# A hybrid decoder layer: order of sums, casts and low parts in the down projections, and place of two norm matmuls

## The chip, the cores and the metric

The kernel runs on one core of a Trainium2 chip. The metric is the time of one execution on the device in microseconds (us), lower is better. Times are medians of several runs.

## The reference, cut to what matters

One inference step of a decoder layer with two feed-forward blocks around a mixing part, in float32, for 1048 tokens (16 learned, 1024 of the prompt, 8 samples) and a model width of 1024:

```
h = h + 0.5 * swiglu(rmsnorm(h, n1), w1g, w1u, w1d)
u = rmsnorm(h, nm) @ w_in
...                      (two scans over u, one output projection)
h = h + 0.5 * swiglu(rmsnorm(h, n2), w2g, w2u, w2d)

def swiglu(x, wg, wu, wd):
    return (jax.nn.silu(x @ wg) * (x @ wu)) @ wd
```

`wg` and `wu` are 1024 x 2816, `wd` is 2816 x 1024. The change concerns the products with `wd`, the two **down phases**, and the norm that follows the first of them.

## The kernel before

**One product in three.** A float32 matmul is done as three in a reduced format (`mm3`, L140 to L145): each operand is split into a high part, the cast of it (L137, on ACT, the scalar engine), and a low part, operand minus high part (L138, on DVE, the vector engine). The three products are high by high (L143), high by low (L144) and low by high (L145), 262 columns (a quarter of the tokens) each. The low part needs the cast, so DVE waits for ACT each time.

**Seven products in place of eight.** `down` (L529) multiplies 2 by 2 blocks with seven products after Strassen and Winograd. Blocks of the weight are its even and odd row tiles by its even and odd column tiles (11, 12, 21, 22), blocks of the hidden activations are token quarters. The products p run in the order 1, 5, 6, 7, 3, 4, 2 (`DORDER`, L468). Four of them need sums of weight blocks (L563): S1 = 21 + 22 for p=5, S2 = S1 - 11 for p=6, S3 = 11 - 21 for p=7, S4 = 12 - S2 for p=3. S1, S2 and S4 share one kept buffer, each written over the one before; S3 is made in the raw buffer of block 11. Sums of activation blocks were stored to DRAM earlier and come back as operands (`Hidden.load`, L509, transfers u<-hd).

**Steps.** The phase is a list of steps on PE (the tensor engine), 24 for each product: four pairs of output tiles j, three groups of weight rows g (4, 4 and 3 tiles of 128), two halves c of the tokens. A step has 12 or 9 matmuls. A **piece** is the weight of one (p, j, g); it serves two steps, and b is the first of them. In the last product (p=2) the order is c, j, g: a piece has one step in each half, pieces are one step apart, and the last six pieces live in larger "u" buffers. `S.before(i, f)` (L286 to L307) puts f ahead of step i. Within `manual_schedule` (L626 and after) the order in which these functions run is the order of the instructions on each engine and on SP, the queue that issues the DMAs. So the numbers in `S.before` are the plan: an engine works through its list in order, waits where data are missing, and runs ahead of PE where nothing holds it.

For a piece: loads at b-13 (L553, raw buffers, 8 of them), the sum, where there is one, at b-8, cast and low part at b-7 (L566 to L568). The split weights lie in 6 buffers "ws" (L71). For an operand: load, then cast and low part in one step s, for most products s = b-16+3m for its six parts m.

**Ends.** After the last step of a pair j, DVE adds 0.5 times the result to the residual stream h (L582): 4 such evacuations in p=1, 2 in p=5, 3 in p=6, 2 in p=7, 1 in the others. PE has two accumulators "acc", so tile j+2 waits for the evacuation of tile j. Where a block of h is final and a norm follows (first phase, from p=3 on), ACT squares it (L198, L201) and POOL (GpSimd) adds the squares up (L202). `Norm.end(q)` (L204 to L209) lets PE add the squares of quarter q over the partitions (matmul with ones, L209), ACT and DVE make the reciprocal root from it (L159 to L163). In the first phase quarters 1 and 3 are final after p=3. `after1` puts their `nm.end` at e3+2 and e3+4 (L1432), where e3 is the first step of p=4. In the second phase no such norm follows; output tiles are transposed and written instead.

Of the kernel before, what the change touches and what calls it, by code (L numbers as in the profile page):

```python
# [9 lines left out]
F32 = mybir.dt.float32  # L10
F32R = mybir.dt.float32r
U8 = mybir.dt.uint8
AF = mybir.ActivationFunctionType
ALU = mybir.AluOpType
# [3 lines left out]
P = 128  # L18
# [194 lines left out]
def new_x(K):  # L213
    K.xhi, K.xlo = ([K.slot("u", T, F32R) for k in range(KT)] for i in range(2))
# [133 lines left out]
def product(K, ps, w, op, n, first, last, more=False):  # L348
    for k in range(n):
        ks = slice(k * Q, k * Q + Q)  # L350
        wh, wl = (w[:, o + k * P : o + k * P + P] for o in (0, 512))
        K.mm3(ps, wh, wl, op[0][:, ks], op[1][:, ks], first and k == 0, last and k == n - 1, more)
# [119 lines left out]
class Hidden:  # L472
# [36 lines left out]
    def load(self, S, p, at):  # L509

        K = self.K
        op = [{}, {}]

        def load(g, c):
            i, n = GROUPS[g]
            op[c][g] = K.slot("u", n * Q, F32R), K.slot("u", n * Q, F32R)
            K.nc.sync.dma_start(op[c][g][1].bitcast(F32), self.d[p][:, c, i : i + n].rearrange("p n t -> p (n t)"))

        def split(g, c):
            hi, lo = op[c][g]  # L520
            K.split(lo.bitcast(F32), hi, lo)

        for (g, c), l, s in zip([(g, c) for g in range(3) for c in range(2)], *at):
            S.before(l, lambda g=g, c=c: load(g, c))
            S.before(s, lambda g=g, c=c: split(g, c))
        return op


def down(K, S, wdv, hidden, src, h, after):  # L529

    nc = K.nc
    s0 = len(S.steps)
    hs = []
    sums, w = {}, {}

    def load_h(o):
        t = K.slot("s", T)
        nc.sync.dma_start(t, src(o))
        h.append(t)
        hs.append(t.rearrange("p (c n t) -> p c n t", c=2, n=2))  # L540

    for o in range(KT):
        S.before(s0 + (-4, 2, 8, 9)[o // 2], lambda o=o: load_h(o))

    def pieces(p, j, g, b, tag):

        i0, n = GROUPS[g]
        raw = {}

        def load(a):  # L550
            i, o = {11: (0, 0), 12: (1, 0), 21: (0, 1), 22: (1, 1)}[a]
            raw[a] = K.raw(n * P)
            nc.sync.dma_start(raw[a].rearrange("p (k c) -> p k c", k=n), wdv[:, 2 * i0 + i : 2 * (i0 + n) : 2, (2 * j + o) * P : (2 * j + o) * P + P])  # L553

        def val(x):
            return raw[x] if x in raw else sums[j, g]

        def sum_(x, y, op):
            if p == 5:
                if (j % 2, g) == (0, 0):  # L560
                    sums["slots"] = [K.slot("u", 1024) for _ in range(3)]
                sums[j, g] = sums["slots"][g][:, j % 2 * 512 : j % 2 * 512 + n * P]
            nc.vector.tensor_tensor(raw[11] if p == 7 else sums[j, g], val(x), val(y), op)  # L563

        def split():
            t = K.ws() if tag is None else K.slot(tag, 1024, F32R)  # L566
            w[p, j, g] = K.split_w(val({1: 11, 7: 11, 4: 22, 2: 12}.get(p, 0)), t)

        for a in {1: (11,), 5: (21, 22), 6: (11,), 7: (11, 21), 3: (12,), 4: (22,), 2: (12,)}[p]:
            S.before(b - 13, lambda a=a: load(a))  # L570
        if p in (5, 6, 7, 3):
            x, y = {5: (21, 22), 6: (0, 11), 7: (11, 21), 3: (12, 0)}[p]
            S.before(b - 8, lambda: sum_(x, y, ALU.add if p == 5 else ALU.subtract))
        S.before(b - 7, split)

    def matmuls(p, j, g, c, op, ps):
        product(K, ps, w[p, j, g], op[c][g], GROUPS[g][1], g == 0, g == 2)

    def post(p, j, cs, b):
        for i, n in {1: ((0, 0), (0, 1), (1, 0), (1, 1)), 5: ((0, 1), (1, 1)), 6: ((0, 1), (1, 0), (1, 1)), 7: ((1, 0), (1, 1)), 3: ((0, 1),), 4: ((1, 0),), 2: ((0, 0),)}[p]:  # L580
            t = hs[2 * j + i][:, cs, n]
            nc.vector.scalar_tensor_tensor(t, b, 0.5, t, ALU.mult, ALU.add)  # L582
        for i, n in {3: ((0, 1), (1, 1)), 4: ((1, 0),), 2: ((0, 0),)}.get(p, ()):
            if then:
                for c in range(cs.start, cs.stop):
                    then(2 * j + i, 2 * c + n)

    for a, p in enumerate(DORDER):
        b = s0 + 24 * a
        if a == 0:  # L590
            at = [b + k for k in (-14, -11, -11, -9, -9, -7)], [b + k for k in (-8, -7, -6, -5, -4, -2)]
        else:
            at = [b - 22 + 3 * m for m in range(6)], [b - 16 + 3 * m for m in range(6)]
        op = hidden.load(S, p, at)
        if a < 6:
            for j in range(KT // 2):
                box = []
                for g in range(3):
                    pieces(p, j, g, b + 6 * j + 2 * g, None)
                    for c in range(2):  # L600

                        def mm(p=p, j=j, g=g, c=c, op=op, box=box):
                            if not box:
                                box.append(K.psum2()[:, :, :Q])
                            matmuls(p, j, g, c, op, box[0][:, c])

                        S.add(mm, (lambda p=p, j=j, box=box: post(p, j, slice(0, 2), box[0])) if (g, c) == (2, 1) else None)
        else:
            then = after(S, h, b - 48 + 24, b + 12, b + 24)
            for j in range(KT // 2):  # L610
                for g in range(3):
                    pieces(p, j, g, b + 3 * j + g, None if j < 2 else "u")
            for c in range(2):
                for j in range(KT // 2):
                    box = []
                    for g in range(3):

                        def mm(p=p, j=j, g=g, c=c, op=op, box=box):
                            if not box:
                                box.append(K.psum()[:, :Q])  # L620
                            matmuls(p, j, g, c, op, box[0])

                        S.add(mm, (lambda p=p, j=j, c=c, box=box: post(p, j, slice(c, c + 1), box[0][:, None])) if g == 2 else None)
# [768 lines left out]
def body(ctx, tc, a, o):  # L1392
    nc = tc.nc
    K = Core(ctx, tc)
# [5 lines left out]
    x = Input(K, a, wn1, ops)  # L1400
# [12 lines left out]
    def after1(S, h, e3, e0, e1):  # L1413
        nm = Norm(K, h)
# [14 lines left out]
                nc.sync.dma_start(hsp[k * P : (k + 1) * P, cs], h[k][:, cs])  # L1429

        for q in (1, 3):
            S.before(e3 + q + 1, lambda q=q: nm.end(q))  # L1432
        S.before(e0, lambda: new_x(K))
        S.before(e0 + 2, lambda: nm.end(0))
        S.before(e0 + 2, lambda: x_mix(0))
# [43 lines left out]
    for c0, w in CHUNKS:  # L1479
        cs = slice(c0, c0 + w)  # L1480
        for i, (hi, lo) in enumerate(opa):
            t = K.t(w)
# [4 lines left out]
    for k in range(KT):  # L1487
        t = K.slot("s", T)
# [4 lines left out]
    for t in kept:  # L1493
        hi, lo = K.slot("u", T, F32R), K.slot("u", T, F32R)
# [78 lines left out]
```

## Time and profile before

| | |
|---|---|
| median of 3 runs | 2185.61 us (2180.0 to 2186.14) |
| the profiled execution | 2182.61 us, its span 2180.8 us |
| mean granted clock of PE | 0.97 |
| first down phase | evacuations (L582) from 534.7 us on |
| second down phase | evacuations to 2166.0 us |
| loads of down weights | 144 of 256 KB and 72 of 192 KB |

PE, DVE, ACT, POOL and SP are the engines named above; PEld is PE's loading of weights. In a group's line stand line of the code, engine, operation, output<-inputs, shape and count, then busy time in us, mean of one in ns, and idle time of the engine just before with what ended most of it. A line of waits has the waiting engine and line, what it waited for, the time in total, how many waits and the longest. A line of a timeline has start and duration in us. A line of windows has for each engine busy time and instructions, then the granted clock of PE (1.00 is full), the busy share of the DMA engines and GB/s.

### The profile page before, as it was taken

Reading aid. Unit: us, or ns where it says so; the run is one execution under the profiler, and the core shown is the slowest. Engines: PE = TensorE matmul, PEld = TensorE weight load, DVE = VectorE, ACT = ScalarE, POOL = GpSimd, SP = SyncE. Lnnn points to the kernel's source line nnn. Section 1 sums busy time; section 2 is a strip of 40 time slices with the busy share of each in tenths; the row PEclk is TensorE's granted clock in tenths of the full one; section 3 lists DMA queues with packets and bytes.
Section 4 is the critical chain, followed back from the end, with each engine's and each line's share of the span. In section 5 each row is a group of like instructions: output and inputs, shape, how many; then the busy total and the mean of one; then the engine's idle time right before and its main releaser. Section 6 shows DMA issues by size and latency. Waiting matters only on the chain.

```text
span 2180.8 us, 38344 instructions
## 1 busy us (share of the span) xinstructions
PE 2029.1 (93%) x15550; PEld 1972.1 (90%) x15550; DVE 1395.1 (64%) x2358; ACT 786.8 (36%) x1415; POOL 137.6 (6%) x175
## 2 busy tenths in 40 slices
PE   3899999999998989889999998969999999999996
PEld 3799999999898989878989987959999999989996
DVE  5566666666777467587455356776666666678773
ACT  5422222223334444463523334443222222323351
POOL 1000000000002110241111010220000000000000
PEclk8999999999999899989999999989999999999998
DMA  3433333337967421262022053312332333587851
GB/s 120 109 90 102 104 91 102 103 91 214 300 201 215 138 82 36 80 184 79 32 70 78 2 172 103 103 60 74 103 105 87 103 103 89 158 274 226 250 170 57
DMA packets 341816, 264.94 MB, mean 121 GB/s; under 512 B 19136, under 2 KB 317888, under 8 KB 341632
## 3 DMA queue, kind: packets, MB, share of 16 engines
q1 hardware_dynamic: 340824, 260.35, 39.6%
q8 instruction: 123, 2.02, 0.4%
q10 hardware_dynamic: 592, 2.10, 0.3%
q14 instruction: 53, 0.43, 0.1%
q0 software_dynamic: 224, 0.04, 0.0%
HBM read 197.03 MB, written 65.47 MB: 120 GB/s over the span
## 4 chain that ended last, share of the span: by engine, by line
PE 72%; DVE 13%; DMA 5%; ACT 4%; issue 3%; POOL 1%; SPq 1%; ACTq 0%; DVEq 0%; POOLq 0%
PE acc L143 22%; PE acc L144 21%; PE acc L145 21%; DVE u L138 2%; DVE s L582 2%; DMA u<-hd 2%; DVE ws L138 2%; PE mis L1248 2%; ACT ws L137 2%; DMA r<-in_w_ffn_down_dram 1%; DVE u L563 1%; ACT u L137 1%; DVE u L261 1%; DVE r L563 1%; PE mis L1287 0%
## 5 line engine op out<-in xcount | busy, mean ns | idle before, releaser
L143 PE MATMUL acc<-u,ws 128*128 128x262 f32 (+2 forms) x4504 | 1328.2, 296 | 61.0 <-DVE s L582 24.8
L144 PE MATMUL acc<-u,ws 128*128 128x262 f32 (+2 forms) x4504 | 1319.1, 293 | 10.6 <-DVE u L138 10.6
L145 PE MATMUL acc<-u,ws 128*128 128x262 f32 (+2 forms) x4504 | 1315.0, 292 | 0.0
L143 PEld LDWEIGHTS acc<-u,ws 128*128 128x128 f32 x4504 | 860.3, 191 | 81.0 <-issue 28.1
L144 PEld LDWEIGHTS acc<-u,ws 128*128 128x128 f32 x4504 | 863.7, 192 | 13.5 <-DVE u L138 12.1
L145 PEld LDWEIGHTS acc<-u,ws 128*128 128x128 f32 x4504 | 859.9, 191 | 0.4
L138 DVE TENSOR_TENSOR ws<-r,ws 128x512 fp32r<-128x512 f32 (+1 forms) x480 | 328.1, 688 | 259.3 <-ACT ws L137 259.3
L137 ACT CAST ws<-r 128x512 fp32r<-128x512 f32 (+1 forms) x480 | 274.8, 611 | 163.4 <-PE acc L145 80.0
L138 DVE TENSOR_TENSOR u<-u,u 128x1048 fp32r<-128x1048 f32 (+1 forms) x116 | 139.2, 1206 | 44.5 <-ACT u L137 44.0
L420 ACT ACTIVATE t<-t 128x524 f32<-128x524 f32 (+1 forms) x46 | 28.7, 623 | 329.1 <-DVE t L419 329.1
L324 DVE TENSOR_TENSOR r<-r,r 128x512 f32<-128x512 f32 x176 | 118.6, 692 | 15.5 <-DMA r<-in_w_ffn_up_dram 14.0
L137 ACT CAST u<-u 128x1048 fp32r<-128x1048 f32 (+1 forms) x116 | 116.1, 1013 | 26.5 <-DMA u<-hd 21.5
L202 POOL TENSOR_TENSOR t<-t,t 128x262 f32<-128x262 f32 x56 | 50.3, 913 | 842.7 <-ACT t L201 842.7
L582 DVE SCALAR_TENSOR_TENSOR s<-acc,s 128x524 f32<-128x524 f32 (+1 forms) x120 | 77.5, 662 | 36.7 <-PE acc L145 35.6
L413 ACT ACTIVATE t<-acc 128x524 f32<-128x524 f32 (+1 forms) x46 | 27.1, 590 | 183.8 <-PE acc L145 183.8
L137 ACT CAST ws<-u 128x512 fp32r<-128x512 f32 (+1 forms) x72 | 42.1, 585 | 121.7 <-DVE u L563 113.7
L409 ACT COPY t<-acc 128x524 f32<-128x524 f32 (+1 forms) x46 | 26.6, 579 | 156.9 <-PE acc L145 156.9
L138 DVE TENSOR_TENSOR ws<-u,ws 128x512 fp32r<-128x512 f32 (+1 forms) x72 | 47.0, 653 | 36.8 <-ACT ws L137 36.8
L419 DVE TENSOR_TENSOR t<-acc,t 128x524 f32<-128x524 f32 (+1 forms) x46 | 31.2, 679 | 59.9 <-PE acc L145 59.9
L427 DVE TENSOR_TENSOR s<-t,t 128x524 f32<-128x524 f32 (+1 forms) x92 | 58.5, 677 | 1.6
L411 DVE TENSOR_TENSOR t<-acc,t 128x524 f32<-128x524 f32 (+1 forms) x46 | 31.3, 680 | 36.0 <-PE acc L145 36.0
L1248 PEld LDWEIGHTS mis<-s,u 128*128 128x128 f32 x320 | 39.2, 198 | 9.6 <-issue 9.5
(344 smaller groups left out, 1631.7 us busy)
## 6 DMA issues: line engine op xcount, KB each, us to landing
hd<-s SPq DMA_DIRECT2D x170, 262.0 KB
r<-in_w_ffn_down_dram SPq DMA_DIRECT2D x144, 256.0 KB
u<-hd SPq DMA_DIRECT2D x56, 524.0 KB
r<-in_w_ffn_gate_dram SPq DMA_DIRECT2D x88, 256.0 KB
r<-in_w_ffn_up_dram SPq DMA_DIRECT2D x88, 256.0 KB
r<-in_w_in_dram SPq DMA_DIRECT2D x56, 256.0 KB
r<-in_w_ffn_down_dram SPq DMA_DIRECT2D x72, 192.0 KB
u<-hd SPq DMA_DIRECT2D x28, 393.0 KB
```

The costliest lines, as they stand in the source:

```text
L137: self.nc.scalar.copy(hi, src)
L138: self.nc.vector.tensor_sub(lo, src, hi.bitcast(F32))
L143: mm(ps, whi, xhi, start=first, stop=False, skip_group_check=more)
L144: mm(ps, whi, xlo, start=False, stop=False, skip_group_check=more)
L145: mm(ps, wlo, xhi, start=False, stop=last, skip_group_check=more)
L202: K.nc.gpsimd.tensor_add(self.sq[q], self.sq[q], t)
L324: nc.vector.tensor_tensor(raw[p], raw[x], raw[y], op)
L411: nc.vector.tensor_add(temp("v", cs), b, temp("z", cs))
L427: nc.vector.tensor_mul(halves(hid[0][:, n * 2 * Q : n * 2 * Q + 2 * Q])[:, cs], temp(f"g{n}", cs), temp(f"u{n}", cs))
L563: nc.vector.tensor_tensor(raw[11] if p == 7 else sums[j, g], val(x), val(y), op)
L582: nc.vector.scalar_tensor_tensor(t, b, 0.5, t, ALU.mult, ALU.add)
L1248: nc.tensor.matmul(ps[:, 64 * c : 64 * c + 64], kg[:, P * c : P * (c + 1)], qv[:, c, :, 1], start=True, stop=True)
```

## The change

In the down phases sum, cast and low part of a weight now stand one step apart: b-9, b-8, b-7 (before: b-8, b-7, b-7). The low part of an operand stands one step after its cast (before: the same step). S3 is made as 22 - S2, which is the same block, from S2 that is kept; so p=7 loads one block for a piece and not two, and S3 is made in the raw buffer of block 22. The norm matmuls of quarters 1 and 3 after the first phase, with what ACT and DVE do on them, stand at e3+8 and e3+10. Nothing else differs.

```diff
-        def split(g, c):
+        def hi(g, c):
             hi, lo = op[c][g]
-            K.split(lo.bitcast(F32), hi, lo)
+            K.nc.scalar.copy(hi, lo.bitcast(F32))
+
+        def lo(g, c):
+            hi, lo = op[c][g]
+            K.nc.vector.tensor_sub(lo, lo.bitcast(F32), hi.bitcast(F32))
...
-            S.before(s, lambda g=g, c=c: split(g, c))
+            S.before(s, lambda g=g, c=c: hi(g, c))
+            S.before(s + 1, lambda g=g, c=c: lo(g, c))
...
-            nc.vector.tensor_tensor(raw[11] if p == 7 else sums[j, g], val(x), val(y), op)
-
-        def split():
-            t = K.ws() if tag is None else K.slot(tag, 1024, F32R)
-            w[p, j, g] = K.split_w(val({1: 11, 7: 11, 4: 22, 2: 12}.get(p, 0)), t)
-
-        for a in {1: (11,), 5: (21, 22), 6: (11,), 7: (11, 21), 3: (12,), 4: (22,), 2: (12,)}[p]:
+            nc.vector.tensor_tensor(raw[22] if p == 7 else sums[j, g], val(x), val(y), op)
+
+        def hi():
+            src = val({1: 11, 7: 22, 4: 22, 2: 12}.get(p, 0))
+            w[p, j, g] = K.ws() if tag is None else K.slot(tag, 1024, F32R)
+            nc.scalar.copy(w[p, j, g][:, : n * P], src)
+            box.append(src)
+
+        def lo():
+            t = w[p, j, g]
+            nc.vector.tensor_sub(t[:, 512 : 512 + n * P], box[0], t[:, : n * P].bitcast(F32))
+
+        box = []
+        for a in {1: (11,), 5: (21, 22), 6: (11,), 7: (22,), 3: (12,), 4: (22,), 2: (12,)}[p]:
             S.before(b - 13, lambda a=a: load(a))
+
         if p in (5, 6, 7, 3):
-            x, y = {5: (21, 22), 6: (0, 11), 7: (11, 21), 3: (12, 0)}[p]
-            S.before(b - 8, lambda: sum_(x, y, ALU.add if p == 5 else ALU.subtract))
-        S.before(b - 7, split)
+            x, y = {5: (21, 22), 6: (0, 11), 7: (22, 0), 3: (12, 0)}[p]
+            S.before(b - 9, lambda: sum_(x, y, ALU.add if p == 5 else ALU.subtract))
+        S.before(b - 8, hi)
+        S.before(b - 7, lo)
...
         for q in (1, 3):
-            S.before(e3 + q + 1, lambda q=q: nm.end(q))
+            S.before(e3 + q + 7, lambda q=q: nm.end(q))
```

## The prediction, made before the result was known

> **What bounds the kernel now.** I read the page first, then PE's waits in the two down phases, then PE's timeline there with the idle time of each instruction, and last DVE's and ACT's timelines around those idle times.
>
> ```profile
> PE 2029.1 (93%) x15550; PEld 1972.1 (90%) x15550; DVE 1395.1 (64%) x2358; ACT 786.8 (36%) x1415; POOL 137.6 (6%) x175
> ...
> L138 DVE TENSOR_TENSOR ws<-r,ws 128x512 fp32r<-128x512 f32 (+1 forms) x480 | 328.1, 688 | 259.3 <-ACT ws L137 259.3
> ```
>
> PE is busy 93% of the span, so only its idle time and its slow stretches can be won: 2180.8 - 2029.1 = 151.7 us idle in the whole program. DVE waits 259.3 us for the cast in front of a low part, but at 64% busy that matters only where PE waits for DVE. PE's waits in the stretch 500 to 790, which holds the first down phase:
>
> ```profile
> PE acc L143 <- DVE s L582: 14.0, 10, 3.7
> PE mis L209 <- POOL t L202: 7.2, 1, 7.2
> ...
> PE acc L143 <- DVE t L417: 0.9, 1, 0.9
> ```
>
> and in 1890 to 2181, the second:
>
> ```profile
> PE acc L143 <- DVE s L582: 15.3, 10, 3.3
> ...
> PE acc L143 <- DVE t L417: 1.0, 1, 1.0
> ```
>
> So PE waits for the evacuations (L582) and, in the first phase, once for 7.2 us for a norm matmul's squares. Where these are, from PE's timeline of the first phase (start, us; in brackets the idle time before):
>
> ```profile
> 523.40 0.36 PE L143 MATMUL acc<-u,ws 128*128 128x262 f32 x1 [0.94 <-DVE t L417]
> 552.65 0.56 PE L143 MATMUL acc<-u,ws 128*128 128x262 f32 x1 [1.98 <-DVE s L582]
> 564.42 0.36 PE L143 MATMUL acc<-u,ws 128*128 128x262 f32 x1 [2.00 <-DVE s L582]
> 573.99 0.36 PE L143 MATMUL acc<-u,ws 128*128 128x262 f32 x1 [1.35 <-DVE s L582]
> 623.26 0.36 PE L143 MATMUL acc<-u,ws 128*128 128x262 f32 x1 [0.91 <-DVE s L582]
> 631.73 0.36 PE L143 MATMUL acc<-u,ws 128*128 128x262 f32 x1 [0.21 <-DVE s L582]
> 640.69 0.36 PE L143 MATMUL acc<-u,ws 128*128 128x262 f32 x1 [0.69 <-DVE s L582]
> 657.20 0.36 PE L143 MATMUL acc<-u,ws 128*128 128x262 f32 x1 [0.19 <-DVE s L582]
> 707.84 1.24 PE L209 MATMUL mis<-t,ones 128*128 128x262 f32 x2 [7.20 <-POOL t L202]
> 748.16 0.56 PE L143 MATMUL acc<-u,ws 128*128 128x262 f32 x1 [3.70 <-DVE s L582]
> ```
>
> and of the second:
>
> ```profile
> 1951.62 0.36 PE L143 MATMUL acc<-u,ws 128*128 128x262 f32 x1 [3.23 <-DVE s L582]
> ...
> 2125.67 0.36 PE L143 MATMUL acc<-u,ws 128*128 128x262 f32 x1 [1.70 <-DVE s L582]
> ```
>
> A full stretch, and those with half-rate clock:
>
> ```profile
> 550.00:560.00 10.00, 8.02 (x54) 7.83 (x53) 5.73 (x9) 2.73 (x4) 0.00 (x0) 0.83 1.08 354
> 560.00:570.00 10.00, 8.00 (x66) 7.82 (x66) 8.45 (x13) 3.42 (x6) 0.00 (x0) 1.00 0.93 256
> ...
> 590.00:600.00 10.00, 10.00 (x84) 10.00 (x84) 8.42 (x13) 5.07 (x7) 0.00 (x0) 1.00 0.95 287
> ...
> 700.00:710.00 10.00, 2.80 (x14) 2.40 (x13) 5.21 (x6) 5.58 (x11) 5.30 (x6) 0.64 0.82 258
> 710.00:720.00 10.00, 10.00 (x71) 9.94 (x71) 4.86 (x10) 5.25 (x10) 0.00 (x0) 0.85 0.23 60
> ...
> 750.00:760.00 10.00, 9.38 (x63) 9.21 (x62) 1.29 (x3) 0.85 (x2) 0.75 (x1) 0.80 0.56 172
> ```
>
> 84 matmuls in 10 us are 0.119 us each: a step of 12 is 1.43 us, a weight tile j (66 matmuls) 7.86 us.
>
> **The change part by part.** *Norm matmuls.* The first stands at e3+2, PE reaches it at 707.84 - 7.20 = 700.64, and waits for this chain:
>
> ```profile
> 703.82 0.69 DVE L582 SCALAR_TENSOR_TENSOR s<-acc,s 128x524 f32<-128x524 f32 x1
> ...
> 705.17 3.31 POOL L202 TENSOR_TENSOR t<-t,t 128x262 f32<-128x262 f32 x4 [3.18 <-ACT t L201]
> ```
>
> Six steps later PE reaches it at 700.64 + 6 x 1.43 = 709.2; the squares were ready at 707.84. So 7.2 us go. The clock was 0.64 and 0.85 around this wait: 71 matmuls where 84 fit lose 13 x 0.119 = 1.5, and about half of the 2.2 us from 707.84 to 710 is lost too, 1.1; that goes with the wait. Gain 9.8. What is queued behind: ACT and DVE, in order, now wait at e3+8 and e3+10 for PE, with the weights up to e3+16 ready; I count nothing. The cover is those eight steps (11 us) of prepared weights; without it the wait returns, 7.2.
>
> *Order on DVE.* No cast, low part or sum is added, and every load keeps its step on SP's queue (24 are missing there, below). A cast takes one of the six weight buffers a step earlier, at b-8; that buffer was read by steps b-12 and b-11, so this costs nothing while pieces are two steps apart. An operand's low part comes a step later; the last one is first used five steps after that, which covers it. In the built program's order a sum was followed directly by its own low part in 64 of 96 cases; now in 48, in the others evacuations or an operand's low part stand between. But each evacuation now has one more sum ahead of it. The late stretch of the first phase:
>
> ```profile
> 559.11 0.69 DVE L563 TENSOR_TENSOR u<-r,r 128x512 f32<-128x512 f32 x1 [2.04 <-DMA r<-in_w_ffn_down_dram]
> ...
> 561.49 2.78 DVE L582 SCALAR_TENSOR_TENSOR s<-acc,s 128x524 f32<-128x524 f32 x4
> 564.18 0.68 DVE L563 TENSOR_TENSOR u<-r,r 128x512 f32<-128x512 f32 x1
> 565.63 0.69 DVE L138 TENSOR_TENSOR ws<-u,ws 128x512 fp32r<-128x512 f32 x1 [0.76 <-ACT ws L137]
> ...
> 571.05 2.79 DVE L582 SCALAR_TENSOR_TENSOR s<-acc,s 128x524 f32<-128x524 f32 x4
> ```
>
> Sum to own low part is 565.63 - 564.18 = 1.45, of it 0.76 bare wait. From the landing at 559.11 the new order runs sum, wait, low part, second sum, evacuation: with 0.6 from start to start for 512 columns (a tenth of the 0.69 overlaps the next: four evacuations show 2.78, but the next operation starts 2.69 later), 559.11 + 0.6 + 0.76 + 0.6 + 0.6 = 561.67, against 561.49: +0.2. That evacuation ends 2.69 later (564.18 - 561.49), at 564.36. From there to the next one it was 571.05 - 564.18 = 6.87; now there is one bare wait less (0.76) and an operand of 1048 columns in place of one of 786 (an estimate of +0.3 by their columns and the 0.69 of 512 columns): 6.4, so 570.8 against 571.05: -0.3. Thus the waits at 552.65 and 564.42 may shrink, but PE meets the evacuation of 571.05 all the same, only 0.3 earlier. The second sum's data landed somewhere before 564.18; I take it as no wait (nearest row: that sum itself didn't wait), the other end is 3.1 us more per phase.
>
> *The wait at 523.40.* DVE ran two operands' low parts shortly before L417:
>
> ```profile
> 519.64 2.40 DVE L138 TENSOR_TENSOR u<-u,u 128x1048 fp32r<-128x1048 f32 x2
> ```
>
> In the new order one operand's low part (2.40 / 2 = 1.2) that stood ahead of L417 comes after it. 0.94 goes, and with it the stores and loads behind that end of the gate phase come 1.0 earlier: 1.0 for each phase, by the waits 0.9 and 1.0.
>
> *Products 5, 6, 7, 3.* DVE is just in time here. Per product two of eight bare waits go: 2 x 0.76 = 1.5 us. By 657 that is over two products, 3 and more, against waits of 0.91 + 0.21 + 0.69 + 0.19 = 2.0: all of it goes, not more, since PE is then full.
>
> *Product 7 from S2.* One load less for each piece: 24 in the program. How often a sum waited for a landing, from the answer for that line:
>
> ```profile
>   DMA r<-in_w_ffn_down_dram: 4.2, 2
> ```
>
> Twice in 96, both in the late stretches, so nothing is gained in product 7; the cover is the sum's other waits.
>
> *The last product.* Before, in order of time:
>
> ```profile
> 740.53 0.51 ACT L137 CAST ws<-r 128x384 fp32r<-128x384 f32 x1 [1.54 <-PE acc L145]
> ...
> 743.32 0.69 DVE L582 SCALAR_TENSOR_TENSOR s<-acc,s 128x524 f32<-128x524 f32 x1
> ...
> 745.33 2.34 DVE L138 TENSOR_TENSOR u<-r,u 128x512 fp32r<-128x512 f32 x3 [1.31 <-ACT u L137]
> 747.59 0.42 DVE L582 SCALAR_TENSOR_TENSOR s<-acc,s 128x262 f32<-128x262 f32 x1
> ```
>
> The cast waits for a weight buffer of PE; then DVE has two weights' low parts and an operand's ahead of the evacuation at 743.32, and after it ACT's squares stand ahead of the next casts (1.31). Now the operand's low part follows that evacuation and two casts precede the squares: 740.53 + 0.51 + 0.47 (384 columns, by the same tenth) + 0.1 + 0.6 = 742.2, evacuation to 742.9, operand 743.8, three low parts 1.7, so the last evacuation starts at 745.5 instead of 747.59. The wait of 3.70 becomes 1.6: gain 2.1. The half-rate clock after it (63 matmuls, less 5 for idle time, where 84 fit: 16 x 0.119 = 1.9; and half of 1.8 us before 750) goes too: 2.8. In the second phase there are no squares; 1.70 becomes 1.5: 0.2.
>
> *A rule of the clock.* The 1.98 us wait of 552.65 was followed by half rate (0.83; 84 - 54 matmuls, less 17 for the idle time, is 13, or 1.6 us), the 2.00 us of 564.42 by 1.00, and after the 1.70 us of 2125.67 the matmul took 0.36, not 0.56. The Trainium skill, "TensorE: Matmul & The Clock Gate", section "What's actually happening", says that the clock halves after a whole idle window of about 3.4 us, and that windows run freely. By that rule a wait of 1.6 us costs no half rate, and the sum stands; by the 552.65 row it may, and the sum is 1.6 to 2.8 less. The trace disagrees with the full window: 1.98 sufficed.
>
> *Sum.* First phase 1.0 + 0.3 + 2.0 + 9.8 + 2.1 + 2.8 = 18.0. Second: 1.0 - 0.2 (PE waits there for the earlier evacuation, row 1951.62) + 2.0 (as in the first) + 0.2 = 3.0. Together 21.0. The profiled execution took 2182.6 (its span 2180.8 and 1.8 around it), so 2161.6 by it; the median of the three runs stands 3.0 above it, at 2185.6, and the forecast is made for such a median: 2164.6.
>
> **The rivals.** *Only the norm pays.* DVE's total work is unchanged, so its waits may just move: then 9.8 goes, 2176. For it: DVE is 8.42 of 10 us busy at 590. Against: 16 bare waits fewer.
>
> *More.* If the shift lets data land earlier as well, the waits at 552.65, 564.42, 573.99 (5.3, less 1.3 counted, and the 1.6 of a half-rate stretch) and in the second phase 3.23 with 1.6 less 0.8 go too: 5.6 + 4.0 = 9.6 more, 2155.
>
> *No change, the norm's stall returns elsewhere.* PE's 7.2 us let DVE, ACT and DMA get ahead; without it PE may wait for product 4's weights. Low parts for e3+6 and e3+8 then came so:
>
> ```profile
> 703.22 0.68 DVE L138 TENSOR_TENSOR ws<-r,ws 128x512 fp32r<-128x512 f32 x1
> ...
> 706.50 0.69 DVE L138 TENSOR_TENSOR ws<-r,ws 128x512 fp32r<-128x512 f32 x1 [1.99 <-ACT ws L137]
> ```
>
> PE would reach those steps at 700.64 + 4 x 1.43 = 706.4 and at 709.2: tight, but in time. If all of it returns, the rest gives 21.0 - 9.8 = 11.2, of which the last product's 4.9, with no lead left, is lost too: 2179 or more.
>
> *Slower.* Sums stand one step nearer to their loads (four steps instead of five). If landings take longer than those four steps (5.7 us; the point from which it decides), every evacuation of the four products with sums waits one step behind its extra sum: 32 x 1.43 = 45.8, against 14.7 for norm and last product: 2217. Against it: 2 of 96 waited.
>
> That the change doesn't do what it says would be the norm still waiting at e3+8: the margin is 709.2 - 707.8 = 1.4 us, and the evacuation ahead is earlier now; it is in the third rival.
>
> **How the numbers follow.** Forecast 0.46 (2158 to 2171: the second sum's landing, 6.2 more, and half rate, up to 2.8, one way; part of "more" the other), only the norm 0.21, more 0.16, no change 0.10, slower 0.07. 2152 to 2178 takes in the first three, about 0.8. A measurement tells about 0.3% (6.6 us) from no change. Faster 0.83: the first three; within 0.3% 0.10; slower 0.07.
>
> **What would show it.** L209 in product 4 without a wait on POOL, and granted clock 1.00 there; no wait before the last steps of the gate phase; no L582 waits between 615 and 660; the wait before the last product's second tile near 1.6 us. The forecast is wrong if a wait over 3 us stands in product 4, if the late stretch after the landing at 559 costs PE more than its 5.3 us, or if the time is above 2179.

## The result and the profile after

| | before | after |
|---|---|---|
| median of 6 runs | 2182.81 us (2177.34 to 2186.14) | 2167.27 us (2162.26 to 2171.6) |
| ratio of times | 1 | 0.9931, 95% interval 0.9916 to 0.9946 |
| profiled execution | 2182.61 us, span 2180.8 | 2171.6 us, span 2169.9 |

The changed kernel is 15.5 us faster by the medians (forecast 21.0), and its time lies in the forecast range of 2152 to 2178. Its profiled execution happens to be the slowest of its six, so two traces laid side by side show only 11.0 us. Three lines in the code have moved: the evacuation is L596 now (it was L582), the sum L568 (L563), the split of a piece L573 (cast, ACT) and L578 (low part, DVE), the split of an operand L521 and L525 (L137 and L138 serve other parts of the program only).

First the page of the changed kernel, engines and the chain of work that ended last:

```profile
PE 2025.8 (93%) x15550; PEld 1970.2 (91%) x15550; DVE 1397.7 (64%) x2358; ACT 786.8 (36%) x1415; POOL 138.7 (6%) x175
...
PE 82%; DVE 8%; DMA 4%; ACT 3%; issue 2%; POOL 1%; SPq 0%; DVEq 0%; ACTq 0%; POOLq 0%
```

Every engine runs as many instructions as before. PE's busy time is 3.3 us shorter (2029.1 before), since fewer of its matmuls run at half rate, and the other 7.6 us between the two spans are idle time of PE. Its waits in the stretch 500 to 780:

```profile
PE acc L143 <- DVE s L596: 11.5, 5, 5.3
PE acc L143 <- ACT u L226: 1.7, 1, 1.7
PE mis L209 <- POOL t L202: 0.7, 1, 0.7
```

and in 1880 to 2171:

```profile
PE acc L143 <- DVE s L596: 15.1, 6, 5.2
```

The norm's 7.2 us and the waits for L417 are gone (the 0.7 at L209 is a later norm matmul, at 773, which waited 0.69 in the kernel before too). Of ten waits for evacuations in each phase five and six are left, but they add up to little less, 11.5 us for 14.0 and 15.1 for 15.3: the longest of them is 5.3 us now. PE's timeline of the first phase shows where they are:

```profile
549.67 0.36 PE L143 MATMUL acc<-u,ws 128*128 128x262 f32 x1 [0.76 <-DVE s L596]
563.71 0.56 PE L143 MATMUL acc<-u,ws 128*128 128x262 f32 x1 [5.30 <-DVE s L596]
734.72 0.39 PE L143 MATMUL acc<-u,ws 128*128 128x262 f32 x1 [2.50 <-DVE s L596]
743.64 0.36 PE L143 MATMUL acc<-u,u 128*128 128x262 f32 x1 [0.62 <-DVE s L596]
754.69 0.39 PE L143 MATMUL acc<-u,ws 128*128 128x262 f32 x1 [2.35 <-DVE s L596]
```

Between 564 and 734 none is left. The three waits of the late stretch (1.98, 2.00, 1.35) have become one of 0.76 and one of 5.30. In the second phase the same happened. The first line below is its longest wait, the second the first wait of its last product:

```profile
1940.01 0.56 PE L143 MATMUL acc<-u,ws 128*128 128x262 f32 x1 [5.21 <-DVE s L596]
...
2111.79 0.39 PE L143 MATMUL acc<-u,ws 128*128 128x262 f32 x1 [1.39 <-DVE s L596]
```

Windows of the first phase, after (columns as in those of before):

```profile
560.00:570.00 10.00, 6.29 (x32) 6.32 (x33) 9.17 (x15) 3.85 (x7) 0.00 (x0) 0.66 0.99 262
...
700.00:710.00 10.00, 10.00 (x81) 9.87 (x80) 3.13 (x5) 5.76 (x10) 0.37 (x1) 1.00 0.55 175
710.00:720.00 10.00, 10.00 (x84) 10.00 (x84) 9.49 (x14) 7.53 (x12) 2.40 (x2) 1.00 0.42 125
...
740.00:750.00 10.00, 9.38 (x77) 9.20 (x77) 0.86 (x2) 1.99 (x3) 2.25 (x3) 1.00 0.45 159
```

The stretch 700 to 720, where PE had 14 and 71 matmuls, is full at clock 1.00, and the half rate after 740 is gone. In its place stands a clock of 0.66 at 560 to 570: 32 matmuls where 84 fit.

**Where the time went, by places.** Both programs run the same matmuls in the same order on PE, but for the norm matmuls that were moved. So the n-th matmul of L143 is the same work in both traces, and the difference of its two start times is how far the changed kernel is ahead at that place. Behind the norm the lead is read where both kernels have done both norm matmuls. Worked out so from the two timelines (in brackets the time in the changed kernel):

| place | ahead, us | won in this part | forecast |
|---|---|---|---|
| in the gate phase (500), nothing changed so far | 0.7 | 0.7 | 0 |
| start of the down phase (522) | 1.9 | 1.2 | 1.0 |
| end of the late stretch (577) | -0.5 | -2.4 | 0.3 |
| end of product 7 (660) | 2.4 | 2.9 | 2.0 |
| after the norm matmuls (715) | 12.2 | 9.8 | 9.8 |
| after the last product (759) | 17.5 | 5.3 | 4.9 |
| in the second gate phase (1893), nothing changed between | 13.3 | -4.2 | 0 |
| start of the second down phase (1897) | 14.5 | 1.2 | 1.0 |
| end of its late stretch (1959) | 10.5 | -4.0 | -0.2 |
| before the waits of its last product (2110) | 13.6 | 3.1 | 2.0 |
| end of the second phase | 11.0 | -2.6 | 0.2 |

The first phase gave 16.8 where 18.0 were forecast, though one of its terms has the wrong sign. What is missing in these two traces is the second phase (-2.3 for 3.0) and the part between the phases, where no instruction was changed.

### The profile page after: what moved, and what is told of

It reads as the page before. It is cut to its first block, busy times and chain, and to the rows that moved or that the text cites. A ratio compares the mean times of both kernels' runs of the same rounds, so it can differ in the third digit from the quotient of the medians.

```text
span 2169.9 us, 38253 instructions
## 1 busy us (share of the span) xinstructions
PE 2025.8 (93%) x15550; PEld 1970.2 (91%) x15550; DVE 1397.7 (64%) x2358; ACT 786.8 (36%) x1415; POOL 138.7 (6%) x175
## 4 chain that ended last, share of the span: by engine, by line
PE 82%; DVE 8%; DMA 4%; ACT 3%; issue 2%; POOL 1%; SPq 0%; DVEq 0%; ACTq 0%; POOLq 0%
PE acc L143 25%; PE acc L144 25%; PE acc L145 24%; PE mis L1262 1%; DMA r<-in_w_ffn_down_dram 1%; DVE s L596 1%; DVE u L261 1%; DVE u L138 1%; DMA u<-hd 1%; DVE s L1276 1%; DVE s L1264 0%; PE mis L1301 0%; DVE ws L138 0%; DMA s<-in_x_prompt_dram 0%; PE mis L1357 0%
## 5 line engine op out<-in xcount | busy, mean ns | idle before, releaser
L143 PE MATMUL acc<-u,ws 128*128 128x262 f32 (+2 forms) x4504 | 1326.4, 295 | 57.8 <-DVE s L596 22.1
L143 PEld LDWEIGHTS acc<-u,ws 128*128 128x128 f32 x4504 | 858.6, 191 | 75.8 <-issue 20.6
L144 PEld LDWEIGHTS acc<-u,ws 128*128 128x128 f32 x4504 | 862.2, 191 | 14.5 <-DVE u L138 12.5
L138 DVE TENSOR_TENSOR ws<-r,ws 128x512 fp32r<-128x512 f32 x396 | 273.0, 693 | 224.3 <-ACT ws L137 224.3
L137 ACT CAST ws<-r 128x512 fp32r<-128x512 f32 x396 | 227.2, 617 | 88.3 <-PE acc L145 64.7
L596 DVE SCALAR_TENSOR_TENSOR s<-acc,s 128x524 f32<-128x524 f32 (+1 forms) x120 | 77.4, 662 | 41.6 <-PE acc L145 40.5
L525 DVE TENSOR_TENSOR u<-u,u 128x1048 fp32r<-128x1048 f32 (+1 forms) x84 | 97.0, 1159 | 8.4 <-ACT u L521 8.0
L573 ACT CAST ws<-r 128x512 fp32r<-128x512 f32 (+1 forms) x84 | 48.0, 582 | 104.8 <-DMA r<-in_w_ffn_down_dram 45.3
L521 ACT CAST u<-u 128x1048 fp32r<-128x1048 f32 (+1 forms) x84 | 83.2, 993 | 1.3 <-DMA u<-hd 1.3
L578 DVE TENSOR_TENSOR ws<-r,ws 128x512 fp32r<-128x512 f32 (+1 forms) x84 | 56.9, 690 | 41.1 <-ACT ws L573 41.1
L573 ACT CAST ws<-u 128x512 fp32r<-128x512 f32 (+1 forms) x72 | 42.1, 584 | 113.1 <-DVE u L568 110.9
L419 DVE TENSOR_TENSOR t<-acc,t 128x524 f32<-128x524 f32 (+1 forms) x46 | 31.2, 679 | 56.0 <-PE acc L145 56.0
L578 DVE TENSOR_TENSOR ws<-u,ws 128x512 fp32r<-128x512 f32 (+1 forms) x72 | 47.3, 657 | 28.7 <-ACT ws L573 28.7
```

The lines of the kernel that those rows point to most:

```text
L137: self.nc.scalar.copy(hi, src)
L138: self.nc.vector.tensor_sub(lo, src, hi.bitcast(F32))
L143: mm(ps, whi, xhi, start=first, stop=False, skip_group_check=more)
L144: mm(ps, whi, xlo, start=False, stop=False, skip_group_check=more)
L521: K.nc.scalar.copy(hi, lo.bitcast(F32))
L525: K.nc.vector.tensor_sub(lo, lo.bitcast(F32), hi.bitcast(F32))
```

## The experiments

The theory after this comparison: the parts of the first phase paid as forecast, except that in the late stretch the waits merged into one that the half-rate clock prolongs, and that is also what the second phase lost there. Its rivals were that norm and order are not two gains but one, that the late stretch is bound by landings of weights or by DVE and not by the clock, and that the loads saved in product 7 paid. Each kernel was run beside the kernel before on the same chip. "Ahead" is again the lead of PE over the kernel before, at the same matmul of the profiled executions. At 500 us, ahead of everything that the edits touch, these leads differ already, from -0.2 to 2.4 (the changed kernel: 0.7); where it matters, this start is named.

### The norm matmuls alone

```diff
 (the kernel before)
-            S.before(e3 + q + 1, lambda q=q: nm.end(q))
+            S.before(e3 + q + 7, lambda q=q: nm.end(q))
```

> The kernel before with the two norm matmuls six steps later and nothing else. Theory (the parts overlap): PE's 7.2 us wait at the norm and the half-rate clock around it go, 10 to 11 us, so about 2172; the waits for evacuations in products 5 to 7 (2.0 us in the first phase) and the one of 0.94 at the end of the gate phase stay. Rival (the wait returns as one for product 4's weights, since DVE is then still late with the last evacuation of product 3): less than 4 us, 2179 or more.

Measured: 2171.1 us (2168.81 to 2175.93) against 2182.0, ratio 0.9949 (0.9931 to 0.9967): 10.9 us. The norm's wait is gone, and PE is 10.3 ahead after both norm matmuls (start -0.2). But the lead is handed on to a place where DVE isn't ready. PE's timeline in the last product of the first phase:

```profile
739.36 0.56 PE L143 MATMUL acc<-u,ws 128*128 128x262 f32 x1 [5.16 <-DVE s L582]
```

That wait was 3.70 in the kernel before; the lead has sunk to 9.4 behind it. The wait in the gate phase (0.94) stays as it was, and so do the waits in products 6 and 7, all four in the second phase and three in the first (0.20, 0.72, 0.19); the first one there, 0.91 in the kernel before, is missing in this trace. So those that stay belong to the order on DVE, and 1.0 of the 2.9 us that products 5 to 7 won in the first phase comes without it.

### The new order alone

```diff
 (the changed kernel)
-            S.before(e3 + q + 7, lambda q=q: nm.end(q))
+            S.before(e3 + q + 1, lambda q=q: nm.end(q))
```

> The changed kernel with the norm matmuls back at their old steps, so only the order of sums, casts and low parts and the smaller loads are new. Theory (the parts overlap): in the changed kernel the last evacuation of product 3 comes 8.1 us earlier and PE reaches the norm 2.3 us earlier, so of the 7.2 us some 1.4 stay without any move of the norm, and too short for a half-rate clock; time about 2168 to 2172. Rival (the parts add up): the wait of 7.2 us and its half rate stay, and 4 to 5 us are won, about 2178.

Measured: 2171.04 us (2165.67 to 2174.04), ratio 0.9944 (0.9924 to 0.9965): 11.0 us. The norm matmuls stand where they stood before the change, and yet PE waits there for 1.25 us, not 7.20:

```profile
699.31 0.71 PE L209 MATMUL mis<-t,ones 128*128 128x262 f32 x2 [1.25 <-POOL t L202]
```

The reason is on POOL's timeline, here that of the same kernel:

```profile
689.79 4.49 POOL L202 TENSOR_TENSOR t<-t,t 128x262 f32<-128x262 f32 x4 [4.08 <-ACT t L201]
696.57 3.38 POOL L202 TENSOR_TENSOR t<-t,t 128x262 f32<-128x262 f32 x4 [2.29 <-ACT t L201]
```

The last four additions of squares start at 696.57; before they started at 705.17. The new order brings the last evacuation of product 3, and with it the squares, 8.6 us forward, while PE itself came there only 2.6 us sooner. So the two parts overlap: alone each gives 11 us, together 15.5, not 22. Ahead after the norm matmuls: 10.3 (norm alone, start -0.2), 10.8 (order alone, start 1.0), 12.2 (both, start 0.7).

### The last loads of the residual stream later

The landing that DVE waits for at 558 stands on SP's queue behind loads of h, the residual stream. Here the last two of these eight loads go out seven steps later.

```diff
 (the changed kernel)
-        S.before(s0 + (-4, 2, 8, 9)[o // 2], lambda o=o: load_h(o))
+        S.before(s0 + (-4, 2, 8, 16)[o // 2], lambda o=o: load_h(o))
```

> The changed kernel with the loads of the last two tiles of the residual stream seven steps later (s0+16 for s0+9), behind the first six weight loads of product 5 in the queue. Theory (the 5.3 us wait before product 5 is for weights that land late because the DMA engines are full): 1.07 MB at 330 GB/s is 3.2 us, so that the first sum of product 5 runs about 3 us earlier, the wait falls to 2 to 3 us in each phase and its half-rate clock goes; 2157 to 2162. Rival (the order of sums ahead of the evacuation is the cause, not the landing): the wait stays at 5 us and the time at 2167.

Measured: 2169.29 us (2159.86 to 2173.97), ratio 0.9933 (0.9911 to 0.9955); not to be told from the changed kernel. The landing did come sooner. DVE's timeline, first the changed kernel:

```profile
558.12 0.69 DVE L568 TENSOR_TENSOR u<-r,r 128x512 f32<-128x512 f32 x1 [0.34 <-DMA r<-in_w_ffn_down_dram]
...
560.78 2.78 DVE L596 SCALAR_TENSOR_TENSOR s<-acc,s 128x524 f32<-128x524 f32 x4
...
569.72 2.78 DVE L596 SCALAR_TENSOR_TENSOR s<-acc,s 128x524 f32<-128x524 f32 x4
```

then this one:

```profile
554.01 0.69 DVE L568 TENSOR_TENSOR u<-r,r 128x512 f32<-128x512 f32 x1 [0.34 <-DMA r<-in_w_ffn_down_dram]
...
556.68 2.78 DVE L596 SCALAR_TENSOR_TENSOR s<-acc,s 128x524 f32<-128x524 f32 x4
...
569.19 0.97 DVE L525 TENSOR_TENSOR u<-u,u 128x786 fp32r<-128x786 f32 x1
```

Landing and evacuation are 4.1 us earlier (1.4 of it is this trace's start, 2.1 for 0.7), and PE's longest wait falls from 5.30 to 3.88, not to the 2 to 3 that were expected. From the start of the down phase to the end of the late stretch PE loses 0.5 us in place of 2.4. But then it waits for another thing, an operand's low part, which now comes a step after its cast:

```profile
570.22 0.39 PE L144 MATMUL acc<-u,ws 128*128 128x262 f32 x1 [1.78 <-DVE u L525]
```

So the landing was one limit there, and the operand's low part, moved by the change, is the next. The forecast had taken that move as covered. The landing at 558 isn't the only one that holds DVE in the changed kernel: just ahead of it DVE stood for a cast, which ACT could start only when its weight had landed.

```profile
555.02 0.51 ACT L573 CAST ws<-r 128x384 fp32r<-128x384 f32 x1 [6.67 <-DMA r<-in_w_ffn_down_dram]
```

```profile
555.57 0.56 DVE L578 TENSOR_TENSOR ws<-r,ws 128x384 fp32r<-128x384 f32 x1 [4.29 <-ACT ws L573]
```

With the last loads of h later this wait is 2.41 us.

### The wait filled, so that the clock stays up

Eighteen matmuls of 128 columns whose result nobody reads are put ahead of step b of product 5, so that PE isn't idle before the long wait.

```diff
 (the changed kernel)
+        if a == 1:
+            def fill():
+                ps = K.psm()
+                for _ in range(18):
+                    nc.tensor.matmul(ps[:, :P], K.ones[1], K.ident, start=True, stop=True)
+            S.before(b, fill)
```

> The changed kernel with 18 matmuls of 128 columns, whose result nobody reads, put on PE where it waits before product 5 in both down phases. Theory (PE loses time there by the half rate after its wait, and without it would be stopped by the next evacuation, which ends at 572.5 where PE now arrives at 574.6): the granted clock stays at 1.00 and 2 us are won in each phase, about 2163. Rival (the half rate costs nothing, since PE waits for DVE anyway): 2167, or later by what the matmuls take.

Measured: 2173.1 us (2170.08 to 2176.62), ratio 0.9954 (0.9939 to 0.9969). On PE's timeline the fills are 36 instructions, two for each matmul of the code:

```profile
557.69 4.18 PE L614 MATMUL mis<-ident,ones 128*128 128x128 f32 x36
...
563.16 0.36 PE L143 MATMUL acc<-u,ws 128*128 128x262 f32 x1 [1.29 <-DVE s L596]
572.90 0.39 PE L144 MATMUL acc<-u,ws 128*128 128x262 f32 x1 [2.40 <-DVE u L525]
```

and the window of the late stretch is at full clock:

```profile
560.00:570.00 10.00, 8.71 (x73) 8.55 (x73) 9.13 (x15) 3.88 (x6) 0.00 (x0) 1.00 0.96 261
```

Nothing was won by it: a wait of 2.40 us for an operand's low part has come in place of the half rate. At the end of the late stretch PE stands level with the kernel before (0.1) where the changed kernel is 0.5 behind, but this trace had 0.8 more at its start: both lose the same in the stretch, 2.6 and 2.4 us. The clock's loss was therefore not the cause that it had seemed: DVE was late for the next thing anyway. This part of the theory falls; what bounds the late stretch is DVE, in its new order and behind its landings.

### The loads of h later, and product 5's operands back in one step

```diff
 (the kernel with the last loads of h later)
-            S.before(s + 1, lambda g=g, c=c: lo(g, c))
+            S.before(s + (p != 5), lambda g=g, c=c: lo(g, c))
```

> The changed kernel with the last residual loads at s0+16, and in product 5 the operands' low parts back in the step of their casts. In the run with the later loads alone PE waited 1.78 and 2.79 us for such a low part (L525) right after the first wait. Theory (that part of the change costs what the later loads win): these two waits go, PE stands 17 to 18 us ahead of the kernel before from the second product of the second phase on, and the time is about 2164. Rival (only the order is changed, the evacuation behind it comes later by the same): PE's place and the time as with the later loads alone, 2167 to 2169.

Measured: 2164.74 us (2162.6 to 2168.53) against 2183.53, ratio 0.9915 (0.9901 to 0.9928): 18.8 us. In the first phase PE's waits are 2.03, 2.09 and 1.14, all for evacuations, with none for an operand there; the lead is 3.1 at the start of the down phase and 2.9 at the end of the late stretch, so the 2.4 us that the changed kernel loses there are all but gone. In the second phase the waits are 2.45, 2.94 and 1.47, and the lead falls from 17.7 to 16.1 where the changed kernel's falls from 14.5 to 10.5. By the traces that is some 4.6 us in both phases; by the medians the kernel is 2.5 us faster than the changed one, which the two intervals don't separate.

### Four loads of h later

```diff
 (the kernel above)
-        S.before(s0 + (-4, 2, 8, 16)[o // 2], lambda o=o: load_h(o))
+        S.before(s0 + (-4, 2, 12, 16)[o // 2], lambda o=o: load_h(o))
```

> As the kernel with the last residual loads later and product 5's operands back, with the third pair of residual loads also later (s0+12 for s0+8), behind the first two weight loads of product 5. Theory (landings set the wait before product 5): its weights land up to 3 us earlier, and the waits of 3.9 and 2.9 us before product 5 fall below 2 us; about 2161. Rival: these residual tiles are then themselves what the evacuation waits for, and nothing is won, 2164 to 2168.

Measured: 2163.22 us (2159.23 to 2166.77), ratio 0.9911 (0.9897 to 0.9924): the lowest median of this study, though its interval can't be told from the one above, and just overlaps with that of the changed kernel. The waits change their places more than their sum, and they didn't fall below 2 us as expected: 4.03 and 1.61 in the first phase, 2.03 and 2.76 in the second.

### Two loads for product 7 again

```diff
 (the changed kernel)
-        for a in {1: (11,), 5: (21, 22), 6: (11,), 7: (22,), 3: (12,), 4: (22,), 2: (12,)}[p]:
+        for a in {1: (11,), 5: (21, 22), 6: (11,), 7: (11, 21), 3: (12,), 4: (22,), 2: (12,)}[p]:
...
-            x, y = {5: (21, 22), 6: (0, 11), 7: (22, 0), 3: (12, 0)}[p]
+            x, y = {5: (21, 22), 6: (0, 11), 7: (11, 21), 3: (12, 0)}[p]
```

(and S3 is made in the raw buffer of block 11.)

> The changed kernel with S3 made from two loaded blocks again (11 - 21), so 24 more loads. Theory: no place of PE differs by more than 0.5 us within product 7 and the next, since sums there wait for no landing. Rival: waits of DVE or PE for the weights of product 7 or 3 come back, over 1 us.

Measured: 2166.9 us in one execution, against a median of 2183.53 of the kernel before beside it. No wait appears in product 7 or 3, and from the start of product 7 to its end the lead grows by 1.8 us in both kernels. The 24 saved loads pay nothing, as forecast.

### The halves of the new order

The operands' low parts back in the step of their casts, the rest of the change kept:

```diff
 (the changed kernel)
-            S.before(s + 1, lambda g=g, c=c: lo(g, c))
+            S.before(s, lambda g=g, c=c: lo(g, c))
```

> The changed kernel with the low parts of all operands back in the step of their casts; weights and norm as changed. Theory: this part alone removes the wait at the end of the gate phase, so 0.9 us come back there, and the wait of 0.8 us before the last tile of product 1 grows to about 2; in products 5 to 7 no wait returns. Rival (this part is also what keeps DVE ahead in products 6 and 7): waits of 0.2 to 0.9 us for evacuations return there.

And the weights back at their old steps, the rest of the change kept:

```diff
 (the changed kernel)
-            S.before(b - 9, lambda: sum_(x, y, ALU.add if p == 5 else ALU.subtract))
-        S.before(b - 8, hi)
+            S.before(b - 8, lambda: sum_(x, y, ALU.add if p == 5 else ALU.subtract))
+        S.before(b - 7, hi)
         S.before(b - 7, lo)
```

> The changed kernel with the weights' sums back at b-8 and their casts at b-7, beside the low parts; operands and norm as changed. Theory: the bare waits of DVE are what cost PE 2.0 us in products 6 and 7, and they return, 0.2 to 0.9 us each; the wait before product 5 shrinks by about 1 us, as one sum less stands ahead of the evacuation. Rival (the operands' part alone suffices): no wait between 615 and 660.

Measured, one execution each beside a median of 2183.53: 2200.9 with the operands back, which is slower than the kernel before, and 2186.47 with the weights back, within the runs of the kernel before. Both keep the norm's move, which alone gave 2171.1. So against that kernel each half of the order costs time by itself, and only both together gain; the leads at the end of product 3 say the same, -7.8 and -5.4 where the norm alone has 0.5 and the changed kernel 2.5. How, is seen from DVE's waits for ACT in 590 to 690, the changed kernel first:

```profile
DVE ws L578 <- ACT ws L573: 15.8, 20, 1.9
DVE u L525 <- ACT u L521: 1.2, 3, 0.4
```

with the operands back:

```profile
DVE u L525 <- ACT u L521: 18.1, 11, 1.8
DVE ws L578 <- ACT ws L573: 7.9, 9, 1.9
```

with the weights back:

```profile
DVE ws L578 <- ACT ws L573: 22.3, 29, 1.3
```

17.0, 26.0 and 22.3 us; in the kernel before it was 19.5. With the operands back the shape of the loss is this, on DVE's timeline:

```profile
625.90 0.55 DVE L568 TENSOR_TENSOR u<-u,r 128x384 f32<-128x384 f32 x1
628.08 1.25 DVE L525 TENSOR_TENSOR u<-u,u 128x1048 fp32r<-128x1048 f32 x1 [1.63 <-ACT u L521]
```

and on ACT's:

```profile
626.56 0.51 ACT L573 CAST ws<-u 128x384 fp32r<-128x384 f32 x1 [3.57 <-DVE u L568]
626.98 1.06 ACT L521 CAST u<-u 128x1048 fp32r<-128x1048 f32 x1
```

ACT, in order, casts the weight first, and this cast waits for DVE's sum. The operand's cast, whose data were there, stands behind it, and DVE, having done the sum, has the operand's low part next: it waits 1.63 us for two casts where a sum's own low part of 384 columns waits 0.66 for one (620.35 in the changed kernel). The wait isn't at a sum's own low part at all. PE falls behind the kernel before from product 5 on, to 9.2 us early in product 4; a wait of 2.93 us for an evacuation at 636.75 is part of it. The wait at the end of the gate phase is back too (0.97 us), so it was the operands' later low parts that had cleared it. With the weights back nothing stands between most sums and the low part that needs them, and PE waits 0.94 and 2.61 us for operands' low parts.

### Additions on POOL beside product 7

Twenty-four additions of 128x262 on POOL that nobody reads are put beside product 7, to see what DVE's work costs with POOL at work.

```diff
 (the changed kernel)
+                for _ in range(4):
+                    nc.gpsimd.tensor_add(aside[0], src, src)
...
+            for m in range(6):
+                S.before(b - 14 + 3 * m, lambda m=m: pool(m))
```

> The changed kernel with 24 additions on POOL (128x262, results unread) beside product 7 in both phases. In the last product three low parts of 512 columns took 2.86 us beside POOL's additions and 1.7 was forecast. Theory (DVE's operations with two inputs slow down beside POOL): in the stretch with the additions single DVE operations of 512 columns take 1.0 to 1.3 us, against 0.68 in the same stretch without. Rival: they stay at 0.68 and the 2.86 us have another cause.

Measured: 2183.35 us in one execution, against 2183.53: all that the change had won is gone. POOL's and DVE's timelines:

```profile
623.50 12.67 POOL L617 TENSOR_TENSOR t<-u 128x262 f32<-128x262 f32 x12 [2.15 <-ACT u L521]
```

```profile
628.36 2.04 DVE L596 SCALAR_TENSOR_TENSOR s<-acc,s 128x524 f32<-128x524 f32 x3
630.31 1.24 DVE L525 TENSOR_TENSOR u<-u,u 128x1048 fp32r<-128x1048 f32 x1
631.47 1.11 DVE L578 TENSOR_TENSOR ws<-r,ws 128x512 fp32r<-128x512 f32 x1
...
635.61 1.11 DVE L568 TENSOR_TENSOR r<-r,u 128x512 f32<-128x512 f32 x1
637.54 0.69 DVE L578 TENSOR_TENSOR ws<-r,ws 128x512 fp32r<-128x512 f32 x1 [0.82 <-ACT ws L573]
638.15 0.68 DVE L568 TENSOR_TENSOR r<-r,u 128x512 f32<-128x512 f32 x1
```

A low part or sum of 512 columns takes 0.91 to 1.11 us while POOL runs and 0.69 as soon as POOL stops (623.50 + 12.67 = 636.2). The evacuation, one of whose two inputs is PE's accumulator, takes 0.70 at 629.69 all the same; it is the last of the three in the row of 628.36, 2.04 us together, as much as the same three without POOL. The low part of 1048 columns at 630.31 takes 1.24, as it does without POOL; there it is POOL's addition beside it that takes longer, 1.63 us where others take 0.62. So the price is paid now by the one engine, now by the other. By 641.74 PE waits 3.04 us for an operand's low part, and the lead at the end of product 7 is -3.8, not 2.4 (at its start 0.7 and 0.6): 6 us lost, since DVE has no time to spare here.

## Why the prediction was near in its sum and wrong in a step

**Norm matmuls: held in place, overlapping in price.** L209 stands in product 4 without a wait, at clock 1.00, and 9.8 us are won at the norm, as forecast. But 9.8 was reckoned with the squares ready at 707.84 as before, and added to what the order gives. The order alone takes 7.20 down to 1.25. It was in reach of the trace: the row of 703.82 is an evacuation that DVE came to late, behind low parts, since PE itself was past it by 700.64. The terms of the sum weren't independent, and each alone is worth 11 of the 15.5.

**Gate phase and products 5, 6, 7, 3: held.** The waits for L417 are gone (1.2 us won in each phase, 1.0 forecast), and no wait for an evacuation stands between 615 and 660 (2.9 us won, in the second phase 3.1; 2.0 forecast). The reason given, fewer sums followed by their own low part, was only half of it. By that count the kernel with the operands back should be better still: it has 24 such pairs, against 64 before and 48 after, and is the slowest of all. What counts is what stands behind what on both engines, DVE and ACT. The first phase's 2.9 hold 1.0 that the norm alone had too.

**The late stretch: this step failed.** "PE meets the evacuation of 571.05 all the same, only 0.3 earlier": DVE's walk was right (landing 558.12 and evacuations at 560.78 and 569.72; with the landing 1.0 earlier the text's figures give 560.7 and 569.8), but PE didn't meet it, so that 2.4 us were lost where 0.3 were to be won. Its wait merged into one of 5.30 us and a half-rate stretch of 6.8 us, of which 5.5 lay in matmuls (half of it lost, 2.75), and PE came to that tile at 574.5, not 572.5. That was more than the 5.3 us named in the forecast as a sign of its failing. Filling the wait showed that the half rate isn't the limit by itself: without it PE waits 2.40 us for an operand's low part. The sentence "the last one is first used five steps after that, which covers it" is what failed there. DVE is late in product 5, and five steps on PE don't cover a DVE that is behind by its evacuations. With the landing earlier and those low parts back, the stretch costs 0.2 us, not 2.4.

**The second phase: its late stretch failed in the same way.** 3.0 forecast, -2.3 measured. The late stretch with its wait of 5.21 us lost 4.0 (3.0 in the trace of the order alone, 0.6 in that of the norm alone, whose second phase is that of before). The end of the gate phase (1.2) and products 6, 7 and 3 (3.1; the norm alone 0.0) gave what was forecast and more. The last product lost 2.6, but so it did with the norm alone (2.6), so this can't be put down to the change. Its waits of over 3 us are as long as before, but by the trace's records of the granted clock 10.2 us of half rate follow them, where it was 3.4. Without that product some 0.3 is left of the 3.0 forecast.

**The last product: the step held, its size was off.** The wait of 3.70 became 2.50, not 1.6. After the change DVE and POOL show there:

```profile
731.46 2.86 DVE L578 TENSOR_TENSOR u<-r,u 128x512 fp32r<-128x512 f32 x3
734.24 0.42 DVE L596 SCALAR_TENSOR_TENSOR s<-acc,s 128x262 f32<-128x262 f32 x1
```

```profile
731.27 2.04 POOL L202 TENSOR_TENSOR t<-t,t 128x262 f32<-128x262 f32 x2 [7.39 <-ACT t L201]
```

Three low parts were put at 1.7 and took 2.86, beside POOL's additions of squares; the experiment on POOL shows that rise by itself. The Trainium skill, "GPSIMD Engine Reference", section "1. Specifications", says that POOL shares its SBUF interfaces with DVE and contends with DVE instructions that have two SBUF inputs; the traces agree, with 1.11 for 0.69 us, and 0.70 us unchanged for the evacuation, which has only one. The trace of before had rows of it (a low part of 786 columns 1.40 us at 700.00, 0.96 at 702.33; and these three low parts themselves, 2.34 at 745.33), and the forecast's 0.6 for a low part left them out. The second phase has no squares there, and its wait is 1.39 (forecast 1.5). The half rate after the wait went as forecast (2.6 us, 2.8 forecast). That the product gave 5.3, more than the 4.9 forecast, is luck: another 1.5 came where no term stood, since the wait of 2.38 at 770.71 was followed by half rate before the change and its counterpart of 2.35 at 754.69 was not.

**The clock.** A wait of 2.50 us was followed by full rate (0.39, and 1.00 in the window of 740), so the sum stood by the rule of the Trainium skill, "TensorE: Matmul & The Clock Gate", section "What's actually happening". Yet the runs don't make 3.4 us of waiting a threshold: half rate followed 1.98 us in the kernel before, and the 2.50 us before the last product's second tile, which eight of the kernels have, were followed by half rate in five of them and not in three. That the windows run freely, as the same section says, fits this: what a wait of 2 to 4 us costs then depends on where it falls. No run moves a wait alone to show it.

**What is left.** 4.2 us were lost between the phases, in work that wasn't touched. The same part gave anything from 6.2 lost to 2.9 won in the traces of the experiments, and by and large it goes along with the granted clock: between the phases 61 us of half rate were recorded before, 65 in the changed kernel, 68 in the trace that lost most (the last loads of h later) and 48 in the one that won most (four loads later). Why it differs stays open. The profiled execution is also 4.3 us above the median of its kernel. So a single lead behind 790 tells little; what is won from place to place within a phase tells more.

**How much of the hit is luck.** The time came within 2.7 us of the forecast's 2164.6, but the gain, 15.5 for 21.0, is 5.5 short: the forecast started from a median of three runs, 2185.6, and the six give 2182.8. Its range is 26 us wide and holds "only the norm" as well. The order alone measured 11.0, and the forecast's terms without the norm add up to 11.2; that too is luck. In that trace 8.2 of the gain lie at the norm, where the forecast had put nothing for the order, and its second phase, put at 3.0, gave nothing.

**The rivals.** "Only the norm pays" falls: the order alone gives 11.0. What "no change" is built on, a stall that returns elsewhere, shows in one place, the last product's 5.16 us with the norm alone; with both parts it doesn't come. "Slower" by sums too near to their loads falls too: between 590 and 690 of the changed kernel no sum waits for a landing. "More" didn't come from this change; two more edits gave medians that are 2.5 and 4.1 us lower, which the intervals hardly tell from the changed kernel.

## What to carry to other kernels

When two edits clear the same stall, don't add their gains: look whether one of them moves the data that the other waits for, and test each alone. Where two in-order engines hand work back and forth (sum on DVE, cast on ACT, low part on DVE), write both orders side by side and see what stands behind each wait on the other engine; half of a reordering can be slower than none. A wait that is removed in front of an engine which is still late comes back as a wait for the next thing that this engine makes; relieve the late engine or the landing it waits for first.

## What the runs showed of the hardware

- DVE's operations with two inputs in SBUF and POOL's additions hold each other up: on DVE up to 1.11 us against 0.68 for 128x512 and 1.40 against 0.97 for 128x786, or else POOL's addition takes 1.63 against 0.62, as beside a DVE operation of 128x1048 that stays at 1.24. The evacuation from PE's accumulator stays at 0.70.
- Half-rate stretches of PE come in lengths of 3.4 us and multiples. After the waits of 5.2 and 5.3 us in the late stretches they lasted 6.8 us; waits of 2.85 and 2.94 us passed without one in two of the experiments, one of 2.03 us was followed by one.
